# A two-network kernel on one core: last feed-forward groups in another order, squares of the norms split, small-tile products in RWKV-7, attention scores by pairs of heads

## The chip, the cores and the metric

The kernel runs on one core of a Trainium2 chip, as one launch. The metric is the device time of a launch in microseconds (us), lower is better; of several runs the median counts. The engines named here: PE (TensorE, matmuls, with its own weight-load row PEld), DVE (VectorE), ACT (ScalarE), POOL (GpSimd) and SP, whose queue issues most DMAs. Each engine works through its own instructions in the order in which the program lists them, and waits on semaphores for the others.

## The reference, cut to what matters

Two networks follow each other on 256 tokens of width 1024. The first has two layers, each a mixer (latent attention and an mLSTM) and a convolutional feed-forward net (FFN). The second has one layer: HGRN2, RWKV-7 and neighbourhood attention side by side, then a mixture of 32 experts. What the change touches:

```python
def _rmsnorm(x, w, eps=1e-6):
    y = x32 * lax.rsqrt(jnp.mean(x32 * x32, axis=-1, keepdims=True) + eps)
def _conv_ffn(h, w_up, conv_w, conv_b, w_down):
    u = _causal_dwconv(h @ w_up, conv_w, conv_b)
    a, val = jnp.split(u, 2, axis=-1)
    return (jax.nn.gelu(a) * val) @ w_down
def rwkv7_scan(...):      # one step, for 4 heads, forwards and backwards
    sa = jnp.einsum('bhvk,bhk->bhv', s, kk_t)
    s = s * w_t[:, :, None, :] - sa[..., None] * ak_t[:, :, None, :] + v_t[..., None] * k_t[:, :, None, :]
# neighbourhood_attention, 8 heads: 256 keys of the grid and 256 of the context
    s_win = jnp.where(in_win[:, :, None, :], s_win + bias, NEG_INF)
    prob = jax.nn.softmax(jnp.concatenate([s_win, s_ctx], axis=-1), axis=-1)
```

## The kernel before

All activations lie transposed (channels on the partitions, 256 tokens along the row). A product with a weight matrix is made of three fp32r matmuls of 128x256 (`mm3`, lines 474 to 476): weight and activation are each split into a high and a low part. Weights come in 1 MB tiles (`raw`) by SP's queue; ACT casts the high part (`hi`, L451) and DVE subtracts the low one (`lo`, L453). Work that fills gaps runs as background generators, which `tick()` advances by their rates; `ada` (L537, a matrix-vector product on DVE) is one of them. The builder then fixes the order of each engine's instructions.

The stages: context, mixer 0, FFN 0, mixer 1, FFN 1, the middle (norms, HGRN2, RWKV-7, attention, the output product `merged`), and the experts, whose weights (`ew`, 192 tiles of 1 MB) stream in until the end.

- **FFN.** `_ffn_order` sets the order of 22 "up" steps in groups of 6, 6, 5 and 5 and of the "down" steps, four for each group. An up is 48 matmuls and then a convolution, a GELU and a split (`facc`, `fgel`, `hidh` on ACT and DVE, `hidl` on POOL); a down takes the `hidh`/`hidl` tiles of a finished group. Before, all four downs of a group stand behind the first two ups of the next one.
- **Norms.** `sumsq` squares x in four pieces on ACT (L574), sums them on PE with a matrix of ones (L585); `rstd` loads an activation table that has both Ln and Exp (`pin`, L554), then takes Ln and Exp (L561, L562). `scale_blocks` (L607 to L611) makes `hhi` and `hlo`, which PE waits for.
- **RWKV-7.** `rwkv` is called for two pairs of heads, j = 0 and 1: on the context as background of FFN 0 and FFN 1, and on the tokens in the middle (`rwkv_lat`, rate `MID_RATES[0]`, after HGRN2 `MID_RATES[4]`). For chunks of 64 it inverts unit triangular 64x64 matrices, eight on each half of the partitions, level by level: `X` (tile `kt`) and its transpose `XT` (tile `at`), masked parts `bt` of the matrix `AT`. Each of levels 1 to 5 makes two `products` (L1424) of 16 matmuls of 64x64 each, with an ACT copy (`y`, L1436) and a DVE subtraction (L1439) and transposition (L1440) behind them: ten products in a call, 40 in a launch. Ahead of them stand transposes of `kr`, `kt`, `at` (L644) and the products L1402.
- **Attention.** `scores` (L1754 to L1769) handles a head, then its two query blocks; the window's mask is added to the bias on POOL (L1755). PSUM has two buffers named `d`; one holds the scores of a (head, block).

Of the kernel before, what the change touches and what calls it, by code (L numbers as in the profile page):

```python
# [12 lines left out]
F32R = mybir.dt.float32r  # L13
# [6 lines left out]
P = 128  # L20
# [16 lines left out]
ADA_RATE, RK_RATE, MID_RATES = (0.8, 0.45, 0.8, 0.45), 0.8, (0.6, 1.0, 1.0, 1.0, 0.6)  # L37
# [143 lines left out]
def _consts2():  # L181
# [28 lines left out]
    for b in (1, 2, 4, 8, 16, 32):  # L210
        same = s // (2 * b) == u // (2 * b)
        lev.append(par(same & (s // b < u // b), same & (s // b > u // b)).reshape(P, -1))
    c.add("rklev", np.concatenate(lev, axis=1))
    c.add("eye2", np.tile(np.eye(64), (2, 1)))
    n, c = c, Vecs()

    qc, kc = t[:, None] % 64, np.arange(64)[None, :]
    w0 = np.clip(qc - 8, 0, 48)
    c.add("nawin", np.where((kc >= w0) & (kc < w0 + 16), 0.0, NEG))
    return k, r, e, n, c  # L220


def prep(inputs):
# [78 lines left out]
    a["rpb"] = np.stack(b).reshape(P, -1)  # L302
# [7 lines left out]
    for group, k in zip(("all", "one", "two", "tri", "moe", "rk", "na"), (*_consts(), *_consts2())):  # L310
# [41 lines left out]
class Net:  # L352
# [216 lines left out]
    def sumsq(self, out, x, adds=True, weighted=None):  # L569

        nc = self.nc
        for i in range(4):
            sq = self.two()
            nc.scalar.activation(sq, x[:, 2 * i : 2 * i + 2, :], AF.Square)  # L574
            if weighted:
                for c in range(2):
                    w = weighted[1][:, 2 * i + c : 2 * i + c + 1].to_broadcast([P, P])
                    nc.tensor.matmul(weighted[0], w, sq[:, c, :], start=i + c == 0, stop=i + c == 4)
# [8 lines left out]
    def rstd_x(self, x, adds=True):  # L587
# [4 lines left out]
        self.rstd(r, ps[:, :T], 1024)  # L592
# [27 lines left out]
    def norms(self, x, norm, scale, shift):  # L620
# [14 lines left out]
        self.rstd(r2, pw[:, :T], 1024, eps2)  # L635
# [366 lines left out]
    def ffn(self, l, fp, x, mod, rk):  # L1002
# [16 lines left out]
        for op in _ffn_order():  # L1019
            n += 1  # L1020
            ps = new.pop(0) if new else self.ps("dy"[n // 2 % 2])
            if op[0] == "u":
# [16 lines left out]
                hh, hl = (fp.tile([P, T], F32R, tag=n, bufs=9, name=self.uid(n)) for n in ("hidh", "hidl"))  # L1039
# [256 lines left out]
    def rwkv(self, rp, j, m, lat):  # L1296
# [117 lines left out]
        X, XT = ti([8, 64], "kt"), ti([8, 64], "at")  # L1414
# [3 lines left out]
        f3 = lambda t: t.rearrange("p (s c) -> p s c", s=8)  # L1418
        units = [(g, p, slice(64 * p, 64 * p + 64)) for g in range(8) for p in range(2)]

# [5 lines left out]

        for l in range(6):
            bt = ti([8, 64], "bt", 2)
            nc.vector.tensor_tensor(f2(bt), f2(AT), lev[:, l, :].unsqueeze(1).to_broadcast([P, 4, P]), OP.mult)
            if l == 0:  # L1430
                nc.vector.scalar_tensor_tensor(XT, bt, -1.0, self.C("eye2").unsqueeze(1).to_broadcast([P, 8, 64]), OP.mult, OP.add)
# [3 lines left out]
            y = ti([8, 64], "y1")  # L1435
            nc.scalar.copy(f1(y), ps)  # L1436
            if l < 5:
                ps = products("a", lambda g, p, r: XT[r, g, :], lambda g, p, r: y[r, g, :])
                nc.vector.tensor_tensor(X, X, f3(ps), OP.subtract)  # L1439
                nc.vector.transpose(f1(XT), f1(X))  # L1440
            else:
                ps = products("a", lambda g, p, r: y[r, g, :], lambda g, p, r: XT[r, g, :])
                nc.vector.tensor_tensor(XT, XT, f3(ps), OP.subtract)
            yield

# [299 lines left out]
    def neighbourhood(self, np_, m):  # L1745
# [4 lines left out]
        def scores(hd):  # L1750

            hs = slice(64 * (hd % 2), 64 * (hd % 2) + 64)
            bias = self.two("twoa").rearrange("p a t -> p (a t)")[:, :384].rearrange("p (x c) -> p x c", c=64)
            nc.sync.dma_start(bias, self.A["rpb"][:, hd * 384 : hd * 384 + 384].rearrange("p (x c) -> p x c", c=64))  # L1754
# [441 lines left out]
```

## Time and profile before

| | us |
|---|---|
| runs before | 1747.9, 1748.63, 1761.38 |
| median | 1748.63 |
| profiled execution, its own time | 1758.49 |
| its span, first to last instruction | 1756.4 |
| PE busy, of the span | 1576.2 (90%) |
| DVE busy | 1118.8 (64%) |
| ACT busy | 758.8 (43%) |

The profiled execution lies 9.86 us above the median. Busy shares are averages over stages of different kinds: which engine limits a stage has to be read from that stage, and a busy PE may run at half its clock.

### The profile page before, as it was taken

The page shows a single profiled execution, that of the slowest core. Times are in us where ns is not written, and L with a number is a line of the kernel's source. Part 1 is how long each engine was busy: PE and PEld are TensorE (multiplying, and loading weights), DVE is VectorE, ACT ScalarE, POOL GpSimd, SP SyncE. Part 2 cuts the span into 40 slices and gives each one's busy share as a digit, 9 for nine tenths or more (in the row PEclk, how much of TensorE's full clock was granted, in tenths as well). Part 3 has the DMA queues.
Part 4 walks back from the last instruction along what each step waited for, and adds up shares of the span by engine and source line. Part 5 has one row for each costly group of instructions (what it writes and reads, how often), then busy time and mean ns, then how long its engine had stood idle before and what let it go on. Part 6 is the DMA issues. An engine that isn't in the chain of part 4 may idle for free.

```text
span 1756.4 us, 32561 instructions
## 1 busy us (share of the span) xinstructions
PE 1576.2 (90%) x13542; PEld 1271.6 (72%) x13542; DVE 1118.8 (64%) x2155; ACT 758.8 (43%) x1259; POOL 72.8 (4%) x77
## 2 busy tenths in 40 slices
PE   4999999999998999999999999999989777776776
PEld 4898999899997899989999899878874312221211
DVE  7989868898897887789889878666652111111011
ACT  3576545764455754556455576553431000000000
POOL 0000000020010000001011001001000000000000
PEclk8899999999999999999999999989989888988878
DMA  9745765666675467466567733223459999999998
GB/s 392 310 159 209 262 246 192 223 216 236 226 263 190 179 247 281 172 230 239 194 224 259 281 138 132 74 76 138 195 212 419 419 416 416 417 417 418 419 416 343
DMA packets 76809, 460.81 MB, mean 262 GB/s; under 512 B 8562, under 2 KB 11122, under 8 KB 28146
## 3 DMA queue, kind: packets, MB, share of 16 engines
q1 hardware_dynamic: 74352, 452.45, 67.1%
q10 hardware_dynamic: 2306, 6.24, 1.0%
q8 instruction: 108, 1.77, 0.4%
q14 instruction: 43, 0.35, 0.1%
HBM read 457.61 MB, written 1.05 MB: 261 GB/s over the span
## 4 chain that ended last, share of the span: by engine, by line
PE 57%; DMA 24%; DVE 12%; ACT 4%; issue 3%; SPq 0%; POOL 0%; DVEq 0%; ACTq 0%; POOLq 0%
DMA ew<-in_wgu 11%; PE d L474 9%; PE d L476 9%; PE d L475 9%; DMA ew<-in_wdown 8%; DVE lo L453 4%; PE y L474 3%; PE y L476 3%; PE y L475 3%; PE a L1424 3%; DVE raw L537 3%; PE d L2079 2%; DMA raw<-in_ws 2%; PE a L2008 1%; ACT hi L451 1%
## 5 line engine op out<-in xcount | busy, mean ns | idle before, releaser
L451 ACT CAST hi<-raw 128x1024 fp32r<-128x1024 f32 x309 | 322.7, 1048 | 295.6 <-PE d L475 173.1
L453 DVE TENSOR_TENSOR lo<-raw,hi 128x1024 fp32r<-128x1024 f32 x309 | 379.9, 1236 | 86.2 <-ACT hi L451 84.8
L474 PE MATMUL d<-hhi,hi 128*128 128x256 f32 x1320 | 387.4, 295 | 13.7 <-ACT hhi L608 10.4
L475 PE MATMUL d<-hlo,hi 128*128 128x256 f32 x1320 | 382.4, 290 | 3.7 <-DVE hlo L611 3.2
L476 PE MATMUL d<-hhi,lo 128*128 128x256 f32 x1320 | 381.4, 289 | 2.4 <-DVE lo L453 2.4
L474 PEld LDWEIGHTS d<-hhi,hi 128*128 128x128 f32 x1320 | 258.4, 196 | 22.1 <-ACT hhi L608 13.4
L475 PEld LDWEIGHTS d<-hlo,hi 128*128 128x128 f32 x1320 | 259.6, 197 | 7.4 <-DVE hlo L611 5.0
L476 PEld LDWEIGHTS d<-hhi,lo 128*128 128x128 f32 x1320 | 259.8, 197 | 4.5 <-DVE lo L453 3.2
L2079 PE MATMUL d<-ew,xe 128*32 128x512 f32 x984 | 167.2, 723 | 53.2 <-DMA ew<-in_wgu 52.8
L537 DVE SCALAR_TENSOR_TENSOR raw<-raw,cb 128x1024 f32<-128x1024 f32 x160 | 195.1, 1232 | 4.7 <-DMA raw<-in_ada 4.3
L2079 PEld LDWEIGHTS d<-ew,xe 128*32 128x32 f32 x984 | 27.0, 117 | 166.8 <-DMA ew<-in_wgu 140.1
L2084 DVE SCALAR_TENSOR_TENSOR moa<-moa,d 128x512 f32<-128x512 f32 x8 | 5.5, 688 | 177.1 <-ACT moa L2083 177.1
L474 PE MATMUL y<-hhi,hi 128*128 128x256 f32 x352 | 100.9, 287 | 0.0
L476 PE MATMUL y<-hhi,lo 128*128 128x256 f32 x352 | 99.9, 284 | 0.0
L475 PE MATMUL y<-hlo,hi 128*128 128x256 f32 x352 | 99.6, 283 | 0.0
L2097 PE MATMUL y<-ew,mht 128*32 128x512 f32 x472 | 70.5, 649 | 31.6 <-DMA ew<-in_wdown 27.3
L2115 DVE SCALAR_TENSOR_TENSOR x<-f,mod_l,x 128x256 f32<-128x256 f32 x32 | 14.0, 479 | 129.6 <-PE f L2111 129.6
L459 POOL TENSOR_TENSOR hidl<-fgel,hidh 128x256 fp32r<-128x256 f32 x44 | 52.6, 1196 | 829.6 <-ACT hidh L458 786.9
L2083 ACT ACTIVATE moa<-d 128x512 f32<-128x512 f32 x8 | 4.8, 597 | 183.4 <-PE d L2079 183.4
L2097 PEld LDWEIGHTS y<-ew,mht 128*32 128x32 f32 x472 | 12.5, 114 | 79.5 <-DMA ew<-in_wdown 60.5
L474 PEld LDWEIGHTS y<-hhi,hi 128*128 128x128 f32 x352 | 67.4, 192 | 0.6
L476 PEld LDWEIGHTS y<-hhi,lo 128*128 128x128 f32 x352 | 67.4, 192 | 0.3
(669 smaller groups left out, 3180.4 us busy)
## 6 DMA issues: line engine op xcount, KB each, us to landing
raw<-in_ws SPq DMA_DIRECT2D x151, 1024.0 KB, 4.9
ew<-in_wgu SPq DMA_DIRECT2D x100, 1024.0 KB, 18.0
raw<-in_ada SPq DMA_DIRECT2D x80, 1024.0 KB, 5.0
ew<-in_wdown SPq DMA_DIRECT2D x46, 1024.0 KB, 19.8
ew<-in_wgu SPq DMA_DIRECT2D x46, 512.0 KB, 13.8
ew<-in_wdown SPq DMA_DIRECT2D x28, 512.0 KB, 12.6
two<-in_wgu SPq DMA_DIRECT2D x20, 256.0 KB, 8.4
two<-in_wdown SPq DMA_DIRECT2D x16, 256.0 KB, 7.9
```

What stands on the lines that cost most here:

```text
L451: f.append(nc.scalar.copy(hi_, raw))
L453: f.append(nc.vector.tensor_tensor(lo_, raw, hi_.bitcast(F32), OP.subtract))
L459: (eng or self.nc.vector).tensor_tensor(lo, src, hi.bitcast(F32), OP.subtract)
L474: nc.tensor.matmul(out, whi, hhi, start=first and i == 0, stop=False, **s)
L475: nc.tensor.matmul(out, whi, hlo, start=False, stop=False, **s)
L476: nc.tensor.matmul(out, wlo, hhi, start=False, stop=last and i == n - 1, **s)
L537: self.nc.vector.scalar_tensor_tensor(w, w, 0.5, c, OP.mult, OP.mult, accum_out=out)
L1424: nc.tensor.matmul(ps[r, g * 64 : g * 64 + 64], l_(g, p, r), r_(g, p, r), start=True, stop=True, skip_group_check=True)
L2008: nc.tensor.matmul(ps[:, k * P : k * P + P], xn[:, i, d : d + P], of(i), start=i == 0, stop=i == 1, skip_group_check=True)
L2079: nc.tensor.matmul(ps[32 * e : 32 * e + 32, :], xe[:, k, 32 * e : 32 * e + 32], w[e], start=k == 0, stop=k == 7, skip_group_check=True)
L2097: nc.tensor.matmul(py[q][32 * e : 32 * e + 32, :], ht[:, f * P + 32 * e : f * P + 32 * e + 32], w[e], start=f == 0, stop=f == 3, skip_grou ...
L2115: nc.vector.scalar_tensor_tensor(x[:, j, :], ps[:, c * T : c * T + T], g2[:, j : j + 1], x[:, j, :], OP.mult, OP.add)
```

## The change

1. `_ffn_order`: in the last group two of the previous group's downs move behind the group's last ups; `hidh`/`hidl` get 10 buffers for 9.
2. `sumsq`: the last piece is squared in two halves, and the table load (`pin`) stands ahead of it in place of in `rstd`.
3. `rwkv`: levels 1 to 5 keep only the 32x32 diagonal blocks of `X`; a product is 32 matmuls of 32x32 (`products32`) in place of 16 of 64x64; copies, subtraction and transposition are half as wide. Level 0 and the last level take four narrow instructions each in place of one, and the last level adds four ACT copies and four DVE copies that put the full matrix together (`XW`).
4. `scores`: a pair of heads for one query block, both `d` buffers at once, the matmuls of the two heads in turn. The mask is put into the bias on the host, so the POOL addition and its constants go.
5. `MID_RATES`: RWKV-7 runs at 0.9 in place of 0.6 beside HGRN2, at 0.25 in place of 0.6 behind it, and at 0.9 once the attention's inputs are made.

```diff
-ADA_RATE, RK_RATE, MID_RATES = ..., 0.8, (0.6, 1.0, 1.0, 1.0, 0.6)
+ADA_RATE, RK_RATE, MID_RATES = ..., 0.8, (0.9, 1.0, 1.0, 1.0, 0.25, 0.9)
...
-        seq += ups[:2] + downs + ups[2:]
+        k = 4 if g < len(FFN_GROUPS) - 1 else 2
+        seq += ups[:2] + downs[:k] + ups[2:] + downs[k:]
...
         for i in range(4):
             sq = self.two()
-            nc.scalar.activation(sq, x[:, 2 * i : 2 * i + 2, :], AF.Square)
+            if i == 3:
+                self.pin()
+                for c in range(2):
+                    nc.scalar.activation(sq[:, c, :], x[:, 6 + c, :], AF.Square)
+            else:
+                nc.scalar.activation(sq, x[:, 2 * i : 2 * i + 2, :], AF.Square)
...
-        self.rstd(r, ps[:, :T], 1024)
+        self.rstd(r, ps[:, :T], 1024, pin=False)
...
-        X, XT = ti([8, 64], "kt"), ti([8, 64], "at")
+        xx, XW = ti([2, 8, 32], "kt"), ti([8, 64], "at")
+        X, XT = xx[:, 0], xx[:, 1]
+        quads = [(g, q % 2, slice(32 * q, 32 * q + 32)) for g in range(8) for q in range(4)]
+        def products32(l_, r_, other=False):
+            ps = self.ps("a")
+            for g, a, r in quads:
+                o = r if not other else slice(r.start + 32 - 64 * a, r.stop + 32 - 64 * a)
+                nc.tensor.matmul(ps[o, g * 32 : g * 32 + 32], l_(g, a, r), r_(g, r), start=True, stop=True, skip_group_check=True)
+            return ps[:, :T].rearrange("p (g c) -> p g c", g=8)
...
-            ps = products("a", lambda g, p, r: bt[r, g, :], lambda g, p, r: X[r, g, :])
+            ps = products32(lambda g, a, r: bt[r, g, half(a ^ last)], lambda g, r: X[r, g, :], last)
...
-        def scores(hd):
-            nc.gpsimd.tensor_tensor(bias, bias, self.C("nawin").unsqueeze(1).to_broadcast([P, 6, 64]), OP.add)
-            for i in range(2):
-                ps = self.ps("d")
-                for n, k in enumerate((kl[hd // 2][hs], self.naK[hs, hd // 2, :])):
-                    nc.tensor.matmul(ps[:, n * T : n * T + T], q[hd // 2][hs, i * P : i * P + P], k, start=True, stop=True,
+        def scores(hp, i):
+            pss = [self.ps("d") for _ in range(2)]
+            for n, k in enumerate((kl[hp], self.naK[:, hp, :])):
+                for ps, r in zip(pss, (slice(0, 64), slice(64, P))):
+                    nc.tensor.matmul(ps[:, n * T : n * T + T], q[hp][r, i * P : i * P + P], k[r], start=True, stop=True,
...
+            rk[1] = MID_RATES[5]
             self.background(self.prefetch(5), OUT_RATES[2])
```

How this moves instructions. PE at the end of FFN 0, before: behind the last up's matmuls (which read `hhi_3488`) PE comes to downs of the last group, over its `hidh` tiles.

```order
L476 MATMUL d_6155<-hhi_3488,lo_6187 128x256
L474 MATMUL y_6233<-hidh_5758,hi_6234 128x256
L475 MATMUL y_6233<-hidl_5759,hi_6234 128x256
L476 MATMUL y_6233<-hidh_5758,lo_6235 128x256
L474 MATMUL y_6233<-hidh_5832,hi_6234 128x256
```

And now: behind the last up (`hhi_3491`) stand 60 matmuls over tiles of the group before (`hidh_5280` and on), and only then the last group's (from `hidh_5931`).

```order
L477 MATMUL y_6248<-hhi_3491,lo_6292 128x256
L475 MATMUL d_6326<-hidh_5280,hi_6291 128x256
L476 MATMUL d_6326<-hidl_5281,hi_6291 128x256
L477 MATMUL d_6326<-hidh_5280,lo_6292 128x256
L475 MATMUL d_6326<-hidh_5380,hi_6291 128x256
```

So two downs stand between the last up and the first matmul that needs its group.

ACT at the norm of FFN 0, before (`rstd` is the norm's factor, `ksq` and `bt` belong to RWKV-7, `bt` with a Tanh):

```order
L574 ACTIVATE two_3480<-x 128x512
L554 ACT_TABLE_LOAD
L561 ACTIVATE rstd_3484<-f_3469,eps_70 128x256
L1312 ACTIVATE ksq_3643<-ksq_3643 128x256
L562 ACTIVATE rstd_3484<-rstd_3484 128x256
L1313 ACTIVATE ksq_3643<-ksq_3643 128x256
L1337 ACT_TABLE_LOAD
L1337 ACTIVATE bt_3665<-a_3669,rkh_3651 128x256
L608 ACTIVATE hhi_3488<-two_3490,mod_75 128x256 x2
```

And now:

```order
L555 ACT_TABLE_LOAD
L452 CAST hi_3558<-raw_3528 128x1024
L452 CAST hi_3588<-raw_3586 128x1024
L579 ACTIVATE two_3482<-x 128x256 x2
L1343 ACT_TABLE_LOAD
L1343 ACTIVATE bt_3668<-a_3672,rkh_3654 128x256
L562 ACT_TABLE_LOAD
L562 ACTIVATE rstd_3488<-f_3471,eps_70 128x256
L1318 ACTIVATE ksq_3646<-ksq_3646 128x256
L563 ACT_TABLE_LOAD
L563 ACTIVATE rstd_3488<-rstd_3488 128x256
```

The first table load went ahead of the squares; RWKV-7's Tanh went between the squares and the Ln, and three table loads stand behind the squares where two stood. The norm of FFN 1 reads the same.

PE in the middle, where RWKV-7's second pair of heads begins, before: its transposes and L1402 products stand together, with two matmuls of the attention's rotation (`y`) in them.

```order
L489 MATMUL d_13987<-hi_14054,hlo_11862 128x256
L1340 MATMUL a_13910<-ma_12105,up_13861 128x256
L644 MATMUL a_13956<-kon_339,mv_1861_12777 128x128 x2
L644 MATMUL a_13960<-kon_339,kr_13894 128x128 x2
L1151 MATMUL y_13974<-two_13972,kon_339 128x512
L644 MATMUL a_14000<-kon_339,kt_13895 128x128 x4
L644 MATMUL a_14018<-kon_339,at_13896 128x128 x4
L1402 MATMUL a_14033<-kr_13894,kt_13895 64x128
L644 MATMUL a_13960<-kon_339,kr_13894 128x128 x2
L1402 MATMUL a_14033<-kr_13894,kt_13895 64x128 x7
L1402 MATMUL a_14043<-kr_13894,at_13896 64x128
```

And now the same pair begins earlier, among the attention's key products (`d`): six of them stand between the first `kr` transposes and the next ones, and 24 more behind the `mv` transposes, ahead of this piece:

```order
L650 MATMUL a_14402<-kon_340,kr_14303 128x128 x2
L475 MATMUL d_14427<-hhi_12207,hi_14430 128x256
L476 MATMUL d_14427<-hlo_12208,hi_14430 128x256
L477 MATMUL d_14427<-hhi_12207,lo_14431 128x256
L475 MATMUL d_14427<-hhi_12207,hi_14430 128x256
L476 MATMUL d_14427<-hlo_12208,hi_14430 128x256
L477 MATMUL d_14427<-hhi_12207,lo_14431 128x256
L650 MATMUL a_14452<-kon_340,kt_14304 128x128 x3
L1157 MATMUL y_14416<-two_14414,kon_340 128x512
L650 MATMUL a_14452<-kon_340,kt_14304 128x128
L650 MATMUL a_14486<-kon_340,at_14305 128x128 x4
L650 MATMUL a_14402<-kon_340,kr_14303 128x128 x2
```

The block was pulled apart and moved ahead, part of it still stands together. For the first pair of heads it went the other way: its transposes and L1402 products, spread among some 130 matmuls before, now stand in one piece of 27 with three other matmuls in it.

## Rows read from the trace of the kernel before

**Rows 1.** The page's slices: busy tenths in 40 slices of 43.9 us.

```profile
PE   4999999999998999999999999999989777776776
PEclk8899999999999999999999999989989888988878
DMA  9745765666675467466567733223459999999998
```

**Rows 2.** Windows by stage: us, busy (instructions) of five engines, PE clock, DMA, GB/s.

```profile
332.00:540.00 208.00, 207.56 (x2083) 201.83 (x2081) 186.78 (x319) 111.68 (x173) 26.83 (x21) 0.99 0.64 230
1016.00:1165.00 149.00, 147.56 (x1913) 132.22 (x1912) 108.82 (x233) 90.35 (x154) 10.22 (x16) 0.99 0.32 116
1165.00:1197.00 32.00, 29.65 (x209) 24.05 (x207) 21.76 (x39) 17.72 (x31) 2.42 (x2) 0.73 0.19 68
1197.00:1290.00 93.00, 91.84 (x1024) 77.66 (x1021) 58.64 (x151) 43.24 (x93) 5.99 (x6) 0.96 0.46 169
1320.00:1750.00 430.00, 326.95 (x1922) 105.16 (x1918) 55.52 (x129) 34.90 (x71) 0.00 (x0) 0.87 1.01 415
```

**Rows 3.** Windows of 10 us in FFN 0, FFN 1, the middle, the experts' start.

```profile
520.00:530.00 10.00, 10.00 (x85) 10.00 (x85) 8.11 (x11) 4.39 (x6) 0.00 (x0) 1.00 0.82 297
540.00:550.00 10.00, 6.90 (x41) 6.50 (x42) 5.05 (x20) 3.33 (x6) 1.53 (x2) 0.83 0.60 224
990.00:1000.00 10.00, 6.65 (x39) 6.13 (x39) 4.90 (x16) 2.95 (x5) 1.90 (x2) 0.83 0.90 310
1180.00:1190.00 10.00, 10.00 (x72) 7.84 (x71) 6.17 (x12) 3.63 (x7) 0.00 (x0) 0.50 0.44 157
1310.00:1320.00 10.00, 10.00 (x80) 4.76 (x78) 0.82 (x2) 0.92 (x2) 0.00 (x0) 0.86 0.47 181
```

**Rows 4.** Timeline, end of FFN 0, PE and ACT: start, us, instruction, [idle before <-releaser].

```profile
535.77 0.28 PE L476 MATMUL d<-hhi,lo 128*128 128x256 f32 x1
...
543.83 0.50 PE L474 MATMUL y<-hidh,hi 128*128 128x256 f32 x2 [1.88 <-ACT hidh L458]
...
543.37 0.41 ACT L458 CAST hidh<-fgel 128x256 fp32r<-128x256 f32 x1 [1.78 <-DVE fgel L1038]
```

**Rows 5.** Timeline of PE in the middle: small matmuls.

```profile
1195.93 1.15 PE L1424 MATMUL a<-kt,bt 64*64 64x64 f32 x32
1197.01 0.39 PE L489 MATMUL d<-hi,hlo 128*128 128x256 f32 x1
...
1186.34 1.92 PE L1402 MATMUL a<-kr,at 64*64 64x128 f32 x16
...
1229.37 0.34 PE L1475 MATMUL a<-rkS,bt 64*64 64x64 f32 x8
```

**Rows 6.** Source view of line L1475: duration ns, min/median/max, of one matmul.

```profile
L1475 PE MATMUL a<-rkS,bt x128: 218/228/267, 435.9 to 1241.4; 64*64 64x64 f32 x128
```

**Rows 7.** Timeline of PE: score matmuls on both halves of the rows, and on one.

```profile
1201.52 0.48 PE L1759 MATMUL d<-naK,y4hi 64*128 64x256 f32 x1
1201.53 0.48 PE L1759 MATMUL d<-y4lo,y4hi 64*128 64x256 f32 x1
1201.84 0.38 PE L1759 MATMUL d<-naK,y4hi 64*128 64x256 f32 x1
...
1209.65 0.70 PE L1759 MATMUL d<-y4lo,y4hi 64*128 64x256 f32 x2
1210.19 0.59 PE L1759 MATMUL d<-naK,y4hi 64*128 64x256 f32 x2
```

**Rows 8.** Timeline of ACT at the norm of FFN 0.

```profile
325.04 0.63 ACT L574 ACTIVATE two<-x 128x512 f32<-128x512 f32 x1
325.69 1.28 ACT L554 ACT_TABLE_LOAD   x1
...
328.50 1.28 ACT L1337 ACT_TABLE_LOAD   x1
...
330.17 1.30 ACT L608 ACTIVATE hhi<-two,mod 128x256 fp32r<-128x256 f32 x3
```

**Rows 9.** Timeline of ACT at the norm of mixer 1.

```profile
557.68 0.63 ACT L574 ACTIVATE two<-x 128x512 f32<-128x512 f32 x1 [0.39 <-DVE x L1048]
...
559.63 0.47 ACT L561 ACTIVATE rstd<-f,eps 128x256 f32<-128x256 f32 x1
```

More of the change, by code (lines that the diff above doesn't have):

```diff
@@ L211, in _consts2 @@
         same = s // (2 * b) == u // (2 * b)
-        lev.append(par(same & (s // b < u // b), same & (s // b > u // b)).reshape(P, -1))
+        lev.append(par(same & (s // b < u // b), same & (s // b > u // b)).reshape(P, -1) * (1.0 if b < 32 else -1.0))
     c.add("rklev", np.concatenate(lev, axis=1))
     c.add("eye2", np.tile(np.eye(64), (2, 1)))
[L215 to L220, printed above, removed]
+    return k, r, e, c
 def prep(inputs):
@@ L309, in prep @@
     cat = {}
-    for group, k in zip(("all", "one", "two", "tri", "moe", "rk", "na"), (*_consts(), *_consts2())):
+    for group, k in zip(("all", "one", "two", "tri", "moe", "rk"), (*_consts(), *_consts2())):
         a["k_" + group] = k.array()
@@ L573, in sumsq @@
             sq = self.two()
-            nc.scalar.activation(sq, x[:, 2 * i : 2 * i + 2, :], AF.Square)
-            if weighted:
+            if i == 3:
+                self.pin()
                 for c in range(2):
-                    w = weighted[1][:, 2 * i + c : 2 * i + c + 1].to_broadcast([P, P])
-                    nc.tensor.matmul(weighted[0], w, sq[:, c, :], start=i + c == 0, stop=i + c == 4)
+                    nc.scalar.activation(sq[:, c, :], x[:, 6 + c, :], AF.Square)
+            else:
+                nc.scalar.activation(sq, x[:, 2 * i : 2 * i + 2, :], AF.Square)
+            for c in range(2 if weighted else 0):
+                w = weighted[1][:, 2 * i + c : 2 * i + c + 1].to_broadcast([P, P])
+                nc.tensor.matmul(weighted[0], w, sq[:, c, :], start=i + c == 0, stop=i + c == 4)
             if adds and i in (1, 2):
@@ L1038, in ffn @@
                 nc.vector.tensor_tensor(g, g, u[1], OP.mult)
-                hh, hl = (fp.tile([P, T], F32R, tag=n, bufs=9, name=self.uid(n)) for n in ("hidh", "hidl"))
+                hh, hl = (fp.tile([P, T], F32R, tag=n, bufs=10, name=self.uid(n)) for n in ("hidh", "hidl"))
                 self.split(hh, hl, g, nc.gpsimd)
@@ L1430, in rwkv @@
             if l == 0:
-                nc.vector.scalar_tensor_tensor(XT, bt, -1.0, self.C("eye2").unsqueeze(1).to_broadcast([P, 8, 64]), OP.mult, OP.add)
+                for q in range(4):
+                    r, c = slice(32 * q, 32 * q + 32), half(q % 2)
+                    nc.vector.scalar_tensor_tensor(XT[r], bt[r, :, c], -1.0, self.C("eye2")[r, c].unsqueeze(1).to_broadcast([32, 8, 32]),
+                                                   OP.mult, OP.add)
                 nc.vector.transpose(f1(X), f1(XT))
                 continue
-            ps = products("a", lambda g, p, r: bt[r, g, :], lambda g, p, r: X[r, g, :])
[L1435 to L1439, printed above, removed]
+            last = l == 5
+            ps = products32(lambda g, a, r: bt[r, g, half(a ^ last)], lambda g, r: X[r, g, :], last)
+            y = ti([8, 64], "y1").rearrange("p (x g) c -> p x (g c)", x=2)[:, 0].rearrange("p (g c) -> p g c", g=8)
+            nc.scalar.copy(y, ps)
+            if not last:
+                ps = products32(lambda g, a, r: XT[r, g, :], lambda g, r: y[r, g, :])
+                nc.vector.tensor_tensor(X, X, ps, OP.subtract)
                 nc.vector.transpose(f1(XT), f1(X))
             else:
-                ps = products("a", lambda g, p, r: y[r, g, :], lambda g, p, r: XT[r, g, :])
-                nc.vector.tensor_tensor(XT, XT, f3(ps), OP.subtract)
+                ps = products32(lambda g, a, r: y[r, g, :], lambda g, r: XT[r, g, :], True)
+                for q in range(4):
+                    r, a = slice(32 * q, 32 * q + 32), q % 2
+                    nc.scalar.copy(XW[r, :, half(a)], XT[r])
+                    nc.vector.tensor_copy(XW[r, :, half(1 - a)], ps[r])
             yield
+        XT = XW
         tile_of = lambda g, p: unit(g % 4, p)[:2]
@@ L1768, in scores @@
                 nc.vector.tensor_scalar(mx, mx, -1.0, None, OP.mult)
[L1769 removed]
+                nc.scalar.activation(s, s, AF.Exp, bias=mx, accum_out=den[:, i, 2 * hp + h2 : 2 * hp + h2 + 1])
                 yield s
[L1772 to L1773 removed]
+        todo = [(2 * hp + h2, i) for hp in range(4) for i in range(2) for h2 in range(2)]
+        ready = (s for hp in range(4) for i in range(2) for s in scores(hp, i))
         s = [next(ready) for _ in range(NA_AHEAD)]
```

25 lines of the change are left out of this document (11 added, 14 removed).

## The prediction, made before the changed kernel was run

> **What bounds the kernel now.** I read the slices of the page first, then windows by stage. PE is at nine tenths nearly everywhere until the experts, where it falls to seven or eight and DMA goes to nine [rows 1]. The stages say it sharper [rows 2]. In FFN 0 PE is busy 207.56 of 208 us, beside HGRN2 147.56 of 149, in the attention 91.84 of 93: there a microsecond of PE is a microsecond of time. From 1320 to 1750 the DMA engines are full (1.01, 415 GB/s) and PE is busy 327 of 430: the experts last as long as their weights take to arrive. Just ahead, at 1310 to 1320, DMA is at 0.47 [rows 3]: the weight buffers are full and the transfers wait for PE to use them up. So whatever is taken off the work ahead of the experts starts the stream earlier and moves the end by as much; nothing in the experts changes.
>
> The profiled execution took 1758.49 us, 9.86 above the median of 1748.63. I make the sum on its rows and take the difference off the median, where the same stretches stand. About 1% (17.5 us) is what a measurement of this kernel can tell from no change.
>
> **A. The ends of the FFNs.** In full work PE gets through 85 matmuls in 10 us, 0.118 us each. In the windows around the ends of FFN 0 and FFN 1 it gets through 41 and 39 [rows 3]: 44 and 46 too few, 5.2 and 5.4 us, 10.6 together, part as standing still, part as the clock (0.83) that follows. The timeline shows the cause: PE stood 1.88 us until ACT had cast `hidh`, and ACT had waited for `fgel` [rows 4]; the last group's downs need the last up's convolution, GELU and split. The last up's last matmul began at 535.77, so the last group's tile took some 8 us to become ready, and PE had only this group's own early tiles to fill them. Now two downs of the group before, 60 matmuls or 7.1 us, stand behind the last up as well, and more than cover the stop with the wait before it. What is late next is DVE, which makes `facc` and `fgel` and has `ada` in its line as well; it is busy 186.78 of 208 us [rows 2], so it may fall behind by the 2 or 3 us of slack that are left. The moved downs lose nothing where they came from, since the ups of the last group stand there. I take 10, with 7 to 10.6 as bounds (7 if one end keeps 3.6).
>
> **B. Products on 32x32 tiles.** Forty products: 20 in the FFNs, 20 in the middle. A product of 16 matmuls of 64x64 with fp32 in two records each, 32 records on two tiles, holds PE from 1195.93 to the next matmul at 1197.01 [rows 5]: 1.08 us, 0.067 for a round of two records. The same with 128 columns takes 1.92 us for 16 records [rows 5] at half clock (0.50 from 1180 to 1190 [rows 3]), 0.24 a round and 0.12 at full clock. Between 64 and 128 columns lies 0.053, which leaves 0.014 that does not depend on columns; with 32 columns a round takes 0.040. If four small tiles work at once, the 64 records of a new product are 16 rounds: 0.64 us, 0.44 less than now. The trace has nothing with 32x32, so the other bound is the row with four tiles in use: eight records in 0.34 us [rows 5], of which the last one takes 0.22 [rows 6], leaving 0.12 for seven starts, 17 ns each. If the start alone sets the time, 64 records take 1.1 us and nothing is gained. I take 0.40, near the first bound since columns and not starts explain both rows of products. In the FFNs that is 8 us, of which I credit 7, because DVE has little to spare there; in the middle 8, of which I credit 5, because the products wait in a chain for ACT's copy and DVE's subtraction. These are half as wide, but PE fills such gaps with other work only where the order gives it some. Level 0 and the last level need some twelve more narrow instructions of DVE and eight copies in each of four calls; they lie on DVE and ACT, of which DVE has 40 us to spare in the 149 beside HGRN2 and 34 of 93 later [rows 2], so I cost them at nothing here, and 1 us a call in the bounds. Credit 12, bounds 0 to 16.
>
> The Trainium skill ("TensorE: Matmul & The Clock Gate", section "Wait — 56ns, not 53.3ns?") says that matmuls never start closer together than about 25 ns. The 17 ns of the row with four tiles speak against it, for tiles that work side by side. By that floor, 64 records would take 1.6 us and a product would cost 0.52 more; that is a rival below.
>
> **C. The hole ahead of the second pair of heads.** From 1165 to 1197 PE's clock is 0.73 and it is busy 29.65 of 32 us [rows 2]: 32 x 0.27 = 8.6 us lost to the clock and 2.35 to standing still, 11.0. The order of before had the second pair's transposes and L1402 products there in one block, where the whole RWKV-7 prologue of that pair was waited for, as nothing else was left to do. Now this prologue is drawn ahead, among key products that can run meanwhile, so PE has work over the same wait. Against it: the first pair's prologue has closed up into one block, and may make a hole of its own. I take 6, bounds 0 and 11.
>
> **D. Scores in pairs.** Two records on the two halves of the rows begin 10 ns apart and the pair is followed after 0.32 us [rows 7]; where a head runs alone two records take 0.53, from 1209.65 to 1210.19 [rows 7]. For the eight score records of two heads that is 4 x 0.53 - 4 x 0.32 = 0.84, and there are 8 such units: 6.7 us if every pair runs side by side. Some pairs ran so already by chance, and the new order leaves some apart, so I take 2.5. Against it, both `d` buffers are held at once, and PE, which needs one for its other products, queues behind: -2, between 0 and -3. The POOL addition that goes was on an engine which nobody waited for; its cost is zero.
>
> **E. Norms.** At FFN 0 a table load stands behind the squares now and two after (three in all behind the pieces of the squares, for two), at 1.28 us each [rows 8]. The squares of the last half end earlier by about 0.3 (half of 0.63), so each FFN norm loses about 0.9, where PE must wait for `hhi`. At the norm of mixer 1 the table load goes in the shade of PE's sums, which is worth at most the 1.3 us between the last square and Ln (557.68 + 0.63 to 559.63 [rows 9]); I take 0.7, and 0.3 for the middle. Net -0.8, bounds -3 and +2.
>
> The skill's page "ScalarE: Activation LUTs" (section "What ACT_TABLE_LOAD costs") gives a switch 2.66 us with its drain. The row shows 1.28 and the next instruction, the cast of `hhi`, begins within 1.7 us of the load's start [rows 8]. By the page each FFN norm would lose 2.3 and not 0.9, and the total would be 2.8 us higher.
>
> **The sum.** 10 + 12 + 6 + 2.5 - 2 - 0.8 = 27.7. 1748.6 - 27.7 = **1721 us**. The last steps of RWKV-7 end some 9 us closer to the first expert by the order; while the weight buffers stay full, that has no price.
>
> **Rivals.**
> - *The hole moves.* The clock and the idle time that C takes out come back around the first pair's prologue, and faster products only make PE wait for DVE and ACT. For it: the closed-up block, and DVE's 187 of 208 us. Then C is 0, B gives 4, D 0, and A stays at 8 to 10: a gain near 12, **1737 us**, within 1%. Chance 0.18.
> - *A floor under starts.* Small records start no closer than 25 ns on any tiles: 64 x 25 = 1.6 us, 40 x 0.52 = 21 us dearer in place of 12 less. The rest gains 15.7 and it ends at **1753 us**. Against it stand the 17 ns. Chance 0.05.
> - *Slower: small records cost what large ones do.* If a record holds PE for as long as one of the product before, 1.08 / 32 = 34 ns, because the four tiles don't work side by side when each has its own weights to load, a product takes 2.2 us: 40 x 1.1 = 44 us dearer, less 15.7: **1777 us**. It decides from 1.08 + 15.7/40 = 1.47 us a product, 23 ns a record; over 1% slower it is from 30 ns. For it: each of the 64 records has a weight load, twice as many as now; against it the eight records of L1475, which have theirs too. Chance 0.05.
>
> **How the numbers follow.** The forecast has the remaining 0.72. The range: with all upper bounds the gain is 10.6 + 16 + 11 + 6.7 + 2 = 46, so 1702; below, A at 8, B at 4 and a lost norm give a gain of 6 or 7, so 1742. That leaves the floor and the slower rival outside, and a little of the forecast's own tail. Faster by over 1% means below 1731: the forecast's case nearly whole and none of the rivals, with a few that swap sides: 0.73. Slower by over 1% needs 30 ns a record: 0.05. The rest, 0.22, is within 1%.
>
> **What would show it.** A: windows at the FFNs' ends with about 85 matmuls in 10 us, and no wait for `hidh`. B: product groups of 64 records in 0.6 to 0.7 us; at 1.1 the credit is gone, at 1.6 or 2.2 a rival holds. C: no stretch of 17 us at half clock in the middle, and no such stretch at the first pair's prologue either. D: score records that begin in twos 10 ns apart, and no wait of PE for a `d` buffer. E: three table loads and Ln behind the last square of the FFN norms. The experts' DMA-bound stretch must keep its 430 us and begin earlier by the gain; if it grows, the sum's first assumption is wrong. The prediction fails if the half-clock stretches, which follow where PE stands still, fall elsewhere, since each 10 us of them costs 5.

## The result, and the profile after

| | median, us | runs |
|---|---|---|
| before | 1749.14 | 20, 1743.92 to 1761.38 |
| changed | 1766.32 | 20, 1756.66 to 1774.75 |

The ratio is 1.0085, with a 95% interval from 1.0068 to 1.0102: 0.85% slower, where 1.6% faster was forecast. The profiled execution of the changed kernel took 1764.32 us, near its median; that of before, 1758.49, lay 9.4 above the median of these runs. So of the 17 us between the medians the two traces show only 5 (spans 1756.4 and 1761.8), and a stage is better read against several traces, as the table of stages further down does.

The slices of the changed kernel's page, beside [rows 1]. In the clock's row the 8 that the middle had before, in the slice from 1142 us, is a 9 now, and the slice from 1189 us has a 7 in place of a 9.

```profile
PE   4999999899998999989999899899989867776776
...
PEclk9999999999999999999999999997989889887888
DMA  9745765566676577566667733142379999999998
```

Windows of the changed kernel for the stages of [rows 2]: us, then busy time (and instructions) of PE, PEld, DVE, ACT and POOL, then PE's clock, the DMA engines' share, GB/s.

```profile
332.00:540.00 208.00, 201.66 (x2378) 195.49 (x2378) 187.93 (x331) 113.99 (x186) 22.77 (x22) 0.98 0.63 221
1016.00:1165.00 149.00, 141.00 (x2208) 125.28 (x2207) 108.01 (x242) 91.91 (x166) 9.10 (x16) 0.99 0.29 100
1165.00:1197.00 32.00, 30.39 (x528) 24.55 (x526) 26.42 (x44) 18.01 (x28) 0.00 (x0) 1.00 0.61 210
1197.00:1290.00 93.00, 88.08 (x1018) 72.66 (x1019) 51.69 (x143) 38.55 (x86) 0.00 (x0) 0.83 0.37 136
1325.00:1755.00 430.00, 328.13 (x1914) 105.49 (x1910) 55.26 (x128) 34.76 (x71) 0.00 (x0) 0.87 1.01 415
```

The experts are as before (430 us at 1.01 and 415 GB/s), as the prediction assumed: the time is made ahead of them. PE is less busy in FFN 0 (201.66 of 208 us, where it was 207.56), beside HGRN2 and from 1197 on. But a shorter busy time is no shorter stage: PE now stands. The hole ahead of the second pair of heads (0.73 in [rows 2]) is gone, 1.00 there, and a new one stands right behind it, 0.83 over 93 us.

What made it is one stop inside one product. PE's timeline of the changed kernel: start, us, instruction, and in brackets the idle time ahead of it and what ended it.

```profile
1197.11 0.34 PE L1440 MATMUL a<-y,kt 32*32 32x32 f32 x19 [0.16 <-DVE kt L1460]
1201.44 0.85 PE L1440 MATMUL a<-y,kt 32*32 32x32 f32 x45 [3.99 <-issue]
1202.22 1.22 PE L1781 MATMUL d<-y4lo,y4hi 64*128 64x256 f32 x2
```

After 19 of 64 equal matmuls, with their operands long there, PE stands for 4 us on "issue": nothing in the trace that it waits for. Two windows of 10 us behind it run at half clock, in all from 1199.4 to 1223.3:

```profile
1200.00:1210.00 10.00, 8.56 (x124) 5.49 (x124) 3.32 (x10) 3.10 (x8) 0.00 (x0) 0.50 0.27 85
1210.00:1220.00 10.00, 10.00 (x154) 7.50 (x154) 3.20 (x8) 3.47 (x12) 0.00 (x0) 0.50 0.08 26
```

A product itself became as short as forecast: 64 records hold PE from 380.79 to 381.47, 0.68 us, beside 1.08 in [rows 5]. But the next product waits half a microsecond for ACT's copy of the one before, which ended at 383.01 (the last line, of ACT's timeline):

```profile
380.79 0.75 PE L1440 MATMUL a<-kt,bt 32*32 32x32 f32 x64
381.47 0.38 PE L475 MATMUL y<-hhi,hi 128*128 128x256 f32 x1
...
383.06 0.42 PE L1440 MATMUL a<-y,kt 32*32 32x32 f32 x28 [0.49 <-ACT y L1456]
...
382.65 0.36 ACT L1456 COPY y<-a 128x256 f32<-128x256 f32 x1
```

In FFN 0 two such waits come to 1.6 us and one stop on "issue" inside a product to 1.3. So from the first down to RWKV-7's first state step it takes 47.4 us there, as before; in FFN 1 it takes 44.8, where it was 47.4.

### The profile page after: what moved, and what is told of

The parts are those of the page before. It is cut to its first block, busy times and chain, and to the rows that moved or that the text cites. A ratio compares the mean times of both kernels' runs of the same rounds, so it can differ in the third digit from the quotient of the medians.

```text
span 1761.8 us, 35149 instructions
## 1 busy us (share of the span) xinstructions
PE 1563.3 (89%) x14822; PEld 1253.8 (71%) x14822; DVE 1122.5 (64%) x2183; ACT 762.8 (43%) x1281; POOL 57.8 (3%) x69
## 5 line engine op out<-in xcount | busy, mean ns | idle before, releaser
L475 PE MATMUL d<-hhi,hi 128*128 128x256 f32 x1288 | 378.9, 296 | 15.7 <-ACT hhi L614 12.4
L477 PE MATMUL d<-hhi,lo 128*128 128x256 f32 x1288 | 371.8, 289 | 5.1 <-DVE lo L454 5.1
L476 PE MATMUL d<-hlo,hi 128*128 128x256 f32 x1288 | 372.8, 290 | 3.5 <-DVE hlo L617 3.3
L476 PEld LDWEIGHTS d<-hlo,hi 128*128 128x128 f32 x1288 | 253.1, 196 | 8.0 <-DVE hlo L617 5.7
L477 PEld LDWEIGHTS d<-hhi,lo 128*128 128x128 f32 x1288 | 252.9, 196 | 7.5 <-DVE lo L454 6.7
L475 PE MATMUL y<-hhi,hi 128*128 128x256 f32 x384 | 109.9, 286 | 0.0
L477 PE MATMUL y<-hhi,lo 128*128 128x256 f32 x384 | 108.8, 283 | 0.7 <-DVE kt L1460 0.7
L476 PE MATMUL y<-hlo,hi 128*128 128x256 f32 x384 | 108.8, 283 | 0.0
L475 PEld LDWEIGHTS y<-hhi,hi 128*128 128x128 f32 x384 | 73.6, 192 | 1.1 <-issue 0.7
L476 PEld LDWEIGHTS y<-hlo,hi 128*128 128x128 f32 x384 | 73.6, 192 | 0.1
```

What stands on the lines that cost most here:

```text
L475: nc.tensor.matmul(out, whi, hhi, start=first and i == 0, stop=False, **s)
L476: nc.tensor.matmul(out, whi, hlo, start=False, stop=False, **s)
L477: nc.tensor.matmul(out, wlo, hhi, start=False, stop=last and i == n - 1, **s)
```

## The experiments

Length of stages in us, from PE's timelines. In an FFN, "norm" goes from the first matmul of its sums of squares to the first down (its `hidl` matmul), "downs" from there to the last; "middle" goes from its first sums of squares to the first expert matmul. One execution each; stages that an edit doesn't touch differ by 1 to 2 us (the middle by up to 4), as the clock falls. "1+5" names the parts of the change that a kernel has.

| kernel | norm 0 | downs 0 | norm 1 | downs 1 | middle | ratio to before [95%] |
|---|---|---|---|---|---|---|
| before | 64.7 | 167.4 | 63.1 | 168.0 | 302.7 | |
| changed (1 to 5) | 65.7 | 165.3 | 66.6 | 165.5 | 308.7 | 1.0085 [1.0068, 1.0102] |
| 1, FFN order | 63.8 | 165.6 | 63.4 | 165.8 | 298.9 | 0.9977 [0.9950, 1.0003] |
| 2, norms | 66.9 | 168.8 | 66.3 | 167.4 | 299.9 | 1.0011 [0.9984, 1.0037] |
| 3, products | 63.4 | 167.1 | 63.2 | 167.3 | 305.6 | 1.0021 [0.9999, 1.0042] |
| 4, scores | 64.9 | 168.2 | 62.8 | 170.2 | 303.1 | 1.0030 [1.0006, 1.0055] |
| 5, rates | 63.8 | 168.2 | 63.2 | 168.0 | 296.0 | 0.9966 [0.9945, 0.9987] |
| all but 3 | 66.8 | 166.2 | 66.4 | 165.2 | 292.3 | 0.9989 [0.9969, 1.0009] |
| 1+5 | 64.6 | 165.7 | 63.9 | 165.6 | 291.6 | 0.9956 [0.9934, 0.9979] |
| 1+5, 3 in FFNs | 64.3 | 163.8 | 63.8 | 163.8 | 290.9 | 0.9935 [0.9911, 0.9959] |
| 1+4+5, 3 in FFNs | 63.4 | 161.7 | 61.4 | 164.2 | 292.3 | 0.9915 [0.9885, 0.9946] |
| 1+2+4+5, 3 in FFNs | 66.2 | 167.3 | 66.0 | 166.4 | 295.3 | 0.9987 [0.9964, 1.0009] |

**Each part by itself.** The edits are the parts of the diff shown above, alone on the kernel before. The FFN order:

> The kernel before with part 1 alone (two downs behind the last ups, 10 buffers). The prediction's theory: the stop at the two FFN ends goes, -10 us, near 1739. Rival, from the milestones of the changed kernel (FFN 0 from the first down to its end 2.1 us shorter, FFN 1 2.6 us): the stop moves ahead to where the last ups or hidden tiles are waited for, -3 us, near 1746; PE's idle time then shows in the 20 us ahead of the FFN's end.

1750.29 against 1755.73 us for before on the same chip, -0.23%, not clear of zero; the downs got 1.8 and 2.2 us shorter. The rival holds. PE's waits from 500 to 556 us, one execution (line, what it waited for: us, times, longest), first of this kernel:

```profile
PE y L476 <- ACT hi L453: 1.4, 1, 1.4
PE d L478 <- DVE lo L455: 1.3, 2, 0.7
```

and of before:

```profile
PE y L474 <- ACT hidh L458: 1.9, 1, 1.9
PE y L475 <- POOL hidl L459: 1.5, 2, 1.1
```

The wait for `hidh` and `hidl` is gone, and one for the split weights `hi` and `lo` has come.

The products:

> The kernel before with part 3 alone (products of 32x32). Prediction: each product holds PE 0.68 in place of 1.08 us, -12 us, near 1737. Rival: the time comes back as stops of PE inside the products, where its next instructions have not arrived (the 64 matmuls and 64 weight loads of a product use up a 16 KB block of code in 1.4 us), and as waits for ACT's copy between them: 0 us where the stops are short, +5 to +10 where one of several us halves the clock; stops of 0.3 to 4 us with no releaser inside the groups of 64 records.

1758.19 against 1755.73, +0.21%: nothing gained, the prediction's -12 is excluded. From the first down to RWKV-7's first state step 2.1 and 2.6 us are saved in the two FFNs, and from there to the last down 1.9 us are lost again in each. PE's waits for DVE's `lo` grew there (0.2 to 1.7 us in FFN 0, 0.9 to 1.6 in FFN 1), beside the old stop for `hidh` and `hidl`, which stayed (3.4 us in FFN 0, 3.0 in FFN 1): work taken off PE ahead of a wait for others lengthens the wait. In the middle the half-clock stretch moved behind a product (1201.4 to 1221.9). In the 20 us ahead of it PE's waits are of 0.51 us at most, so such a stretch does not need a stop of several us.

The norms:

> The kernel before with part 4 alone (last square split, table load ahead of it). Prediction: FFN norms lose 0.9 each, mixer 1 gains 0.7, -0.8 to 0 us. Rival from the milestones of the changed kernel: from the norm's first sums to the first down FFN 0 is 1.0 us longer and FFN 1 3.5 us longer, so +3 to +4 us, near 1752.

1758.63 against 1755.73, +0.11%, with an interval of 4.7 us to both sides; the trace shows 2.2 and 3.1 us for the two norms, the rival's side. ACT's timeline of the changed kernel at the norm of FFN 0, to be read beside [rows 8]:

```profile
325.87 0.81 ACT L579 ACTIVATE two<-x 128x256 f32<-128x256 f32 x2 [0.49 <-DVE x L991]
326.70 1.28 ACT L1343 ACT_TABLE_LOAD   x1
327.99 0.47 ACT L1343 ACTIVATE bt<-a,rkh 128x256 f32<-128x256 f32 x1
328.48 1.28 ACT L562 ACT_TABLE_LOAD   x1
...
330.57 1.28 ACT L563 ACT_TABLE_LOAD   x1
...
332.50 0.45 ACT L1343 ACTIVATE bt<-a,rkh 128x256 f32<-128x256 f32 x1
333.13 1.31 ACT L614 ACTIVATE hhi<-two,mod 128x256 fp32r<-128x256 f32 x3 [0.18 <-DVE two L613]
```

From the end of the squares to `hhi` it is 6.45 us, where it was 330.17 - 325.67 = 4.5: 1.28 for the third load, 0.45 for a second `bt` of RWKV-7 that now stands ahead of `hhi`, and 0.18 of waiting for DVE. (The first `bt` and both `ksq` stood ahead of `hhi` before, too.) PE's wait for `bt`, further on in the norm's stage, grew as well, from 2.6 to 3.8 us in each FFN.

The rates:

> The kernel before with part 5 alone (RWKV-7 spread anew). Prediction: -6 us, near 1743, no long stretch at half clock ahead of the second pair. Rival (the hole moves): another stretch of 15 to 25 us at half clock in the middle, 0 to +8 us, near 1753.

1748.63 against 1755.73, -0.34%, or 6 us by the ratio: the prediction's term. From 1160 to 1240 us no window falls under 1.00:

```profile
1160.00:1180.00 20.00, 18.76 (x137) 14.80 (x136) 17.52 (x30) 17.29 (x26) 1.01 (x1) 1.00 0.39 141
1180.00:1200.00 20.00, 18.81 (x275) 16.42 (x275) 16.47 (x27) 6.78 (x14) 1.02 (x1) 1.00 0.65 232
```

The scores by pairs:

> The kernel before with part 2-free, only the scores by pairs of heads (part 4 of the change). Prediction: +0.5 gain (2.5 saved, 2 lost to the d buffers), -0.5 us. Rival: PE waits for both d buffers at once, +3 us or more; then waits at the score matmuls on DVE or ACT show in the attention.

1757.91 against 1750.49, +0.30%. No score matmul waits for anything by the trace, and the middle is 0.4 us longer than that of before; the rest of what is measured stands in no row. The last run below comes back to it.

**Which parts spoil each other.** The sum of the five ratios is +0.05%, the whole is +0.85%. So four combinations followed.

> The changed kernel with the products of 64x64 back. If the code supply of the 32x32 products is what turns the gain of the rates into the hole at 1197 to 1223, this ends 10 to 15 us below the changed kernel, at or under the kernel before, and shows no stop of several us inside a product. If the hole comes from the spreading or the scores, it stays within 5 us of the changed kernel.

1749.48 against 1750.49: 0.96% or 17 us below the changed kernel, as the first reading expected, and no stop inside a product. The 32x32 products cost 4 us on the kernel before (not clear of zero), and 17 on the kernel with the other four parts.

> The kernel before with parts 1 and 5 (FFN order and rates), the two that gained alone. If they add up: -4 - 6 = -10 us against before. If the gain of one hides the other: -5.

1743.31 against 1750.49, -0.44%; -0.57% would be the sum, which the interval holds. They add up as far as can be told.

> Parts 1 and 5, and the 32x32 products only in the two FFNs (on the context), where the 10 products saved 2.2 to 2.6 us in each up to the last RWKV-7 step; the middle keeps 64x64. If that saving reaches the end: 4 to 5 us below the kernel with parts 1 and 5 alone. If the FFN's end gives it back, as it did where the products changed alone (+1.9 us at each): no difference.

1739.35, -0.65%; the edit is a branch that takes the old code where `lat` is set:

```diff
+            if lat:
+                ps = products("a", lambda g, p, r: bt[r, g, :], lambda g, p, r: X[r, g, :])
...
+                    nc.vector.tensor_tensor(XT, XT, f3(ps), OP.add)
+                yield
+                continue
             ps = products32(lambda g, a, r: bt[r, g, half(a ^ last)], lambda g, r: X[r, g, :], last)
```

With the stop at the FFN's end out of the way, the products' saving reaches the end: downs 1.9 and 1.7 us shorter, the medians 4 us apart (the intervals overlap).

> The changed kernel with 64x64 products in the middle alone (32x32 stays in the FFNs). If the loss is made in the middle: 12 to 17 us below the changed kernel and 3 to 4 below the one with 64x64 everywhere (about 1746). If the FFNs' products cost as well: as the one with 64x64 everywhere or above it.

1749.68 against 1750.65, 0.9987: 0.98% below the changed kernel, all from ten products in each of two calls. The loss is made in the middle. It isn't 3 to 4 us below the kernel with 64x64 everywhere, though: with the split norms the FFNs' products do not gain.

**Why a product stops.** PE's instructions come in blocks: the page's queue of them moved 118 blocks of 16 KB. In the changed kernel PE stops at 1102.7, 1107.1 and 1111.2 and goes on at 1104.9, 1108.2 and 1111.6; its rows between one restart and the next are 256 both times, 255 matmuls and weight loads and one semaphore instruction. Counted on in steps of 256, PE begins a block at 1194.46 and at 1201.44 too. PE's timeline at the three restarts:

```profile
1104.92 0.45 PE L1642 MATMUL f<-hsm,hg 64*64 64x64 f32 x7 [1.97 <-issue]
...
1108.22 0.31 PE L1440 MATMUL a<-y,kt 32*32 32x32 f32 x12 [0.97 <-issue]
...
1111.59 0.52 PE L1440 MATMUL a<-y,kt 32*32 32x32 f32 x37 [0.18 <-issue]
```

A block of 16 KB landed at 1103.49, 1106.85 and 1110.18, so 1.4 us ahead of each restart; all six places inside products where one matmul starts over 0.3 us behind the last go on 1.24 to 1.54 us after a block's landing. Read this way, the blocks can feed 256 rows in 3.4 us, 75 a us. An old product needs 64 rows in 1.08 us, 59 a us; a new one 128 in 0.68, 188 a us. The half microsecond ahead of 383.06 above is not of this kind, although a block had landed at 381.73, 1.33 us earlier: by the same count a block ends at 383.51, inside that product, and PE does not stop there. The Trainium skill ("Runtime: NRT & Kernel Launch", section "Instruction fetch mechanics") has the same blocks, 256 instructions in 16 KiB, fetched by the sequencer while it works on the one before, and calls the cost of a block's end mostly hidden; the traces agree on the size, and show from 0.2 to 4 us where the rows are dense.

The first run on this thins the rows out:

> The changed kernel with each 32x32 product issued in two halves of 32 matmuls, between which other work may stand, so that PE needs its instructions less densely; nothing is computed otherwise. Code supply: the stops inside products shrink and it ends 5 to 15 us below the changed kernel, with the 4 us stop and the half-clock stretch at 1199 to 1223 gone or shorter. If the products' chain through ACT and DVE is what costs: no gain or a few us slower, since a product takes longer to finish.

```diff
-            for g, a, r in quads:
+            for n, (g, a, r) in enumerate(quads):
+                if n == 16:
+                    yield
...
-            ps = products32(
+            ps = yield from products32(
```

1777.87 against 1750.65, 1.0141: slower than the changed kernel. The FFNs' products have no gap in them any more, and the last score comes 31 us earlier than in the changed kernel. But a product now takes two turns of the background work, so RWKV-7's chain fell behind and ran on alone to 1300, with two long half-clock stretches (1270 to 1281, 1284 to 1335), and a third (1181 to 1202) began while PE waited 7.5 us for the load of `up`; its one long gap (2.3 us at 1270.1) stands where its products follow each other without other work. The middle is 330.3 us. The gaps inside products speak for the code supply, but the time is set by the chain's pace and by these stretches, so the run settles nothing for the 4 us stop.

At that stop the block came late: PE went on with the last block at 1194.46 and the next one began at 1198.95, 4.5 us later, not 1.1 as three times between 1104 and 1113. Two expert weight tiles had been issued at 1193. The DMA view of the changed kernel from 1193.2 to 1198.9, with no instruction block in it, and from there on:

```profile
DMA  6630000990410369999896959598997969696969
...
q1 hardware_dynamic: 273, 1.86, 89.9%
...
ew<-in_wgu SPq DMA_DIRECT2D x2, 1024.0 KB, 6.5
```

```profile
DMA  0973990777793733979300000000000000300003
...
q8 instruction: 1, 0.02, 2.8%
```

The next run was to take this transfer away:

> The changed kernel, with only 64 of 2048 columns of the first three expert weight tiles fetched (the rest zero: leaves out part of the weights' values), so that the transfers that fill the DMA engines at 1194 to 1200 shrink. If the 4.0 us stop is a fetch of instructions that waits behind them: the longest stop inside a product near 1.5 us as elsewhere, no half-clock stretch of over 10 us at 1199 to 1223, RWKV-7's last step some 10 us earlier, 8 to 14 us off the time. If the stop comes from the products themselves or from RWKV-7's order: it stays at 4 us.

```diff
+        if self.eloads <= 3:
+            nc.sync.dma_start(w[0][:, :64], src[:, :64])
+            nc.gpsimd.memset(w[0][:, 64:], 0.0)
+            return [t[:, c : c + 512] for t in w for c in range(0, n, 512)]
```

1767.26 against 1753.42, 1.0086, as the changed kernel; the stop stayed (4.26 us of idle time). But the edit had cut other tiles: two of 1 MB still were issued at 1195.6, and the block again began as they ran out, at 1201.61. It tells nothing against the theory and nothing for it. So `<= 6`:

> As the run before with the tiles cut, but for the first six expert tiles (leaves out part of their values): the two that are issued at 1195 and fill the DMA engines until the instruction block comes are among them. If the block waits behind them: it comes some 1 to 1.5 us after PE resumed and the stop is 1 to 1.5 us, no half-clock stretch of 24 us follows, RWKV-7's last step is 8 us or more earlier than in the changed kernel. If not: the 4 us stop stays.

1754.50 against 1756.44, 0.9999 [0.9972, 1.0027], 0.86% or 15 us below the changed kernel. The two transfers are now 32 KB each, the block begins 1.14 us after PE had gone on (1206.34, 1207.48), and the stop is 0.70 us. PE's timeline, and the windows behind it:

```profile
1208.98 0.34 PE L1440 MATMUL a<-y,kt 32*32 32x32 f32 x19 [0.16 <-DVE kt L1460]
1210.02 0.59 PE L1440 MATMUL a<-y,kt 32*32 32x32 f32 x45 [0.70 <-issue]
```

```profile
1210.00:1220.00 10.00, 9.78 (x246) 7.18 (x247) 5.99 (x17) 4.81 (x14) 0.00 (x0) 1.00 0.29 93
1220.00:1230.00 10.00, 9.77 (x224) 8.22 (x210) 5.26 (x12) 5.51 (x14) 0.00 (x0) 1.00 0.13 29
```

The same 19 records, then the same cut; no half clock. From the first score to the second pair's first state step (L1475 of before) it is 32.2 us in place of 44.0; with 64x64 products in the middle it is 32.5. So the late block and what follows it make that stretch long, and by the ratio nearly the whole loss. The edit also leaves out some 6 MB of transfers, but not where time was to be gained: the experts take 445.0 us from their first matmul to the end, 444.0 in the changed kernel, and with half as much left out, in the run before, the time did not move. (This profiled execution was 12 us above its own median, late from the FFNs on and 5 us slower ahead of the scores, with half clock from 1117 to 1124 and from 1178 to 1185; so its whole middle, 302.5 us, shows only 6 of the 15.)

**What limits the FFN's end now.** The multiplication of `ada` on DVE was cut from 1024 to 128 columns, once with the new FFN order and once without:

```diff
-        self.nc.vector.scalar_tensor_tensor(w, w, 0.5, c, OP.mult, OP.mult, accum_out=out)
+        self.nc.vector.scalar_tensor_tensor(w[:, :128], w[:, :128], 0.5, c[:, :128], OP.mult, OP.mult, accum_out=out)
```

> The kernel with the new FFN order alone, and ada's multiplications on DVE cut from 1024 to 128 columns (leaves out seven eighths of the modulation's sums). If DVE's line sets the new wait at the FFN ends (weights' lo and hi late): the stretch from the first down to the last of each FFN gets 2 to 4 us shorter than with the new order alone, and PE's waits for hi and lo there vanish. If the weights' transfers set it: unchanged.

> The kernel before with the same cut of ada (leaves out seven eighths of the modulation's sums). The stop for hidh at the FFN ends stays if it comes from the order: first down to last down within 1.5 us of before. If it shrinks by several us, DVE and not the order made that stop as well.

1723.86 and 1729.06 against 1750.65. With the new order the downs take 160.9 and 160.9 us, 4.7 and 4.9 less than with all of `ada`, and no wait for `hi`, `lo` or `hidh` is left between 500 us and the end of the FFN. With the old order they take 163.5 twice, 3.9 and 4.5 less than before. Both came out on the side of DVE's line, the first by more than was expected: it makes the whole new wait, and it also made most of the old stop, which came down from 3.4 to 1.5 us (`hidh` 0.6, `hidl` 0.9). The order by itself is worth 2.6 us an FFN.

**The scores and the norms.**

> Parts 1 and 5, 32x32 products in the FFNs alone, and the scores by pairs. It stands between the 1739 of the kernel without the pairs and the 1750 of the one with pairs and split norms. If the pairs cost what they did alone: +5, 1744 to 1745. If the norms make all of the difference of 10: 1740.

1738.39 against 1753.42, 0.9915 [0.9885, 0.9946]. So the pairs cost nothing here (-0.2%, the intervals overlap), and what they cost alone, +0.30%, belongs to no row and didn't come again. The difference of 0.72% to the same kernel with split norms, 12.6 us, is the norms'. The table shows where: norms 2.8 and 4.6 us, downs 5.6 and 2.2, middle 3.0. That is more than the norms cost alone. One piece of it can be named: with the Tanh moved, RWKV-7's first L1402 products stand at 362.7 and not 348.6, so the later products meet a block's end, and ACT's other work, at another place. In the kernel with split norms PE stops in the last product of its first inversion, and not in the one without:

```profile
404.38 0.74 PE L1444 MATMUL a<-y,kt 32*32 32x32 f32 x62
407.51 0.26 PE L1444 MATMUL a<-y,kt 32*32 32x32 f32 x2 [2.39 <-issue]
```

A half-clock window from 406.4 to 413.2 follows it, and PE waits 0.9 us for ACT's copies ahead of it. From the first down to the first state step that kernel takes 50.2 us, the one without 44.8: that is 5.4 of the 5.6. The middle's 3.0 us and the 2.2 of FFN 1 stay unexplained; one execution of each is not enough for them.

## Why the prediction was wrong

The forecast was 27.7 us faster; the measurement is 15 us slower by the ratio (17 by the medians). Term by term:

- **A, ends of the FFNs: right in kind, mis-sized.** 10 was taken, 7 to 10.6 bounded; alone it measured 4, not clear of zero (the downs 1.8 and 2.2 us shorter). In the changed kernel the windows of [rows 3] at the two ends have 73 and 68 matmuls, not the 85 that were named as the sign. The wait for `hidh` went, and "what is late next is DVE" came true, but its slack was put at 2 or 3 us on the strength of 186.78 of 208 us busy [rows 2]. That share is a mean over the stage: from 505 to 520 and from 535 to 540 DVE was full before the change too, and the cut of `ada` shows 4.7 us an FFN in it.
- **B, products: the price was right, the credit is the step that failed.** 0.64 us was worked out for a product, 0.68 came. The credit of 12 assumed that PE would always have the next instruction. The rounds, the tiles and the chain through ACT and DVE were all weighed; the code was not, though the number of rows doubles while their time falls. The chain was there too: in FFN 0 of the changed kernel 1.6 us of ACT's copies and 1.3 of a block's end took the whole saving. In the FFNs it gained 4 us once A was in; in the middle ten products in each of two calls cost 16 to 17 us, by one late block, its stop and the 24 us at half clock behind it. The bounds of 0 to 16 had no room below zero, and the trace gave no reason for that. The prediction's last sentence had said what would break it, half-clock stretches that fall elsewhere; what makes PE stand there it had not.
- **C, the hole: right, alone.** 6 taken, 6 measured. In the whole change it was lost again to the half clock behind the late block. That the spread put the second pair's products under the weight transfer isn't shown: with the products alone they run beside the same two transfers (issued at 1194). "The hole moves" was the rival whose picture came nearest, for another reason (it named the first pair's prologue), but its 1737 lies 29 us too low: it kept A at 8 to 10 and B at a gain of 4.
- **D, scores: the net is right** within what can be told: 0.5 us of gain was forecast, -0.2% to +0.3% of the time measured, of both signs. Its two halves were not: no wait for `d` shows, and in the changed kernel only 8 pairs of score records of 32 begin within 20 ns of each other, where 2 did before.
- **E, norms: wrong in size and reach.** 0.9 us an FFN norm was taken; the row of ACT has 1.95, and the stages 2.2 and 3.1. The count had the third load; it missed the second `bt` ahead of `hhi`, PE's longer wait for `bt`, and what the moved Tanh does to RWKV-7 behind it: its chain starts 13 us later. That the stages lie near the 2.3 us of the prediction's other price is luck: a load took 1.28 us, and the next instruction began 1.29 after its start (326.70, 327.99). In company with A, C, D and the FFNs' products E cost 12.6 us.
- **The outer frame held.** The experts kept their 430 us and moved by what came before. The "slower" rival asked for 30 ns a record; records keep 11 ns (0.68 / 64), which ends the rival of a floor of 25 ns too. So the sign came out on that rival's side by a mechanism that was not on the list.

The kernel with the parts 1, 4 and 5 and the small products in the FFNs alone beats both: 1738.39 us, 0.9915 of before.

## What to carry to other kernels

A change that makes instructions shorter and more numerous has a price that no duration shows: divide rows by time and compare it with what the instruction queue brings, and look at what else the DMA engines do there. A wait that is covered hands over to the next engine in line; its slack is read from windows of a few us at that place, not from its share of the stage. And where a part gains alone, try it in company: here the products gained 4 us in the FFNs beside the new order and the rates, and all of them cost 17 beside the other four parts.

## What the runs showed of the hardware

- PE's instructions arrive in blocks of 16 KB, 256 of its rows each. When PE uses them faster than they come, it stops at a block's end and goes on 1.24 to 1.54 us after the next has landed (changed kernel); with idle DMA engines a block came every 3.4 us (1103 to 1111).
- A block waits behind weight transfers: in the changed kernel it began 4.5 us after PE had gone on, with two transfers of 1 MB under way, and 1.14 us after with 32 KB in their place.
- The trace puts such stops down as "issue". A wait for ACT's copy that looks alike (383.06) is told from them by counting rows in steps of 256 from a known block's end.
- A stretch of 20 us at half clock came behind a stop of 4 us (1199.4 to 1223.3), and in the kernel with the products alone with waits of 0.51 us at most in the 20 us ahead (1201.4 to 1221.9).
- Four tiles of 32x32 with 64 records take 0.68 us at full clock and 1.01 at half (the product at 1217.99), and records start 11 ns apart on average at full clock.
